# Order, pairing and banks of the probability-value products in two attention layers

## The chip, the cores and the metric

The kernel runs on one core of a Trainium2 chip. The metric is device time in microseconds (us) of one execution, from the start of the program to its end. Everything is one program: four layers of a first network (layers 0 to 3), then a second block ("mixers", then a feed-forward part), all for 256 latent and 256 context tokens of width 1024.

## What is computed

Layers 0 and 3 are a grouped-query attention with a window. Sixteen query heads of width 64 share four key/value heads; a block of 128 queries looks at up to 512 keys (256 of the context, 256 of the latent tokens). Cut to what the change touches:

```python
# reference, window_gqa_mixer (layers 0 and 3)
logits = jnp.einsum('bqkgd,bjkd->bkgqj', q_b, k_b).astype(jnp.float32) * scale
p = sink_softmax(jnp.where(mask, logits, NEG_INF), sink_l)
o = jnp.einsum('bkgqj,bjkd->bqkgd', p.astype(v_b.dtype), v_b)     # probabilities times values
y = (o * jax.nn.silu(z)) @ w_out
```

Layer 0 computes this for the context tokens (stream `c`, 256 keys) and the latent tokens (stream `l`, 512 keys); layer 3 for the latent tokens only. Everything is in float32.

## The kernel before, in words

**Order of work.** The program is written with a tile framework: the Python text gives a program order, and a scheduler at build time turns it into one fixed instruction list for each engine. At each step it takes, for an engine, the earliest instruction of the program order that is ready by its model; so work that stands later in the text (projections of the next group of heads, of the gate `z`, of the output, or of the next layer) is drawn forward into the gaps of work that stands earlier. On the chip each engine follows its list strictly and waits on semaphores.

**Attention of one layer.** `gqa` (L775 on) first projects keys, values and the first half of the queries, then calls `attend(0, ...)`, projects the second half of the queries, calls `attend(1, ...)`, then multiplies with the gate (`z_mul`, L737 on) and projects the output. `attend` loops over the streams, over two blocks of 128 queries (`q`), and over two key/value heads (`kv`) of the group `g`. For each `kv`:

- `softmax` (L860 on) writes the logits of four query heads into banks of the pool tag `S` (L876, L877; L880 adds the mask), takes the maximum (L881), the exponential (L889) and normalises (L897).
- For each tile of 128 keys (`j`; four for stream `l`, two for `c`), four transposes (L910) turn the probabilities of the four heads into a bank with tag `tp`; `evac` copies that bank to an SBUF tile `pT` (tag `T2`, three slots; ScalarE L704 and VectorE L708 in turn); two products (L915) multiply it with the values and add into the output bank `o`. The trace shows each product as two MATMUL instructions, and the tile `pT` under the name `T`.
- After both `kv`, `evac` copies `o` to the tile of `z` (named `Z` in the trace).

A product has 64 output columns of values, so its two heads of `i` go to the lower and the upper 64 partitions of `o`: in the trace these MATMULs have the shape `128*64`, all others around them `128*128`.

**Banks.** PSUM has eight banks here, shared out by tag: three `mm` (projections), two `S` (logits), three `tp` (transposes, the sums of the modulation weights at L518, and `o`). A projection fill is 48 matmuls of 256 columns or 24 of 512 (lines L377, L378 and L380, or L366 to L368) into one `mm` bank; a gate projection is then read once by ScalarE (L747) and once by VectorE (L748), after which its bank is free.

**Counts.** Layer 0: 2 groups x (2 blocks x 2 heads x 2 key tiles for `c` + 2 x 2 x 4 for `l`) = 48 tiles `pT`. Layer 3: 2 x 2 x 2 x 4 = 32. Together 80, with two products each.

Of the kernel before, what the change touches and what calls it, by code (L numbers as in the profile page):

```python
# [19 lines left out]
F32 = mybir.dt.float32  # L20
# [40 lines left out]
class Weight:  # L61


    def __init__(self, name, src, K, blocks, kstep, rows=None, pick=None):
        self.name, self.src, self.K, self.kstep, self.rows, self.pick = name, src, K, kstep, rows, pick
        self.blocks = blocks
        self.off = []
        off = 0
        KC = K // 128
        for cols in blocks:  # L70
            parts = []
            for k0 in range(0, KC, kstep):
                kc = min(kstep, KC - k0)
                parts.append((off, k0, kc, len(cols)))
                off += 128 * kc * len(cols)
            self.off.append(parts)
        self.size = off
# [191 lines left out]
class Net:  # L269
    def __init__(self, tc, A, out, stack, upto=99):  # L270
        self.tc, self.nc, self.A, self.out = tc, tc.nc, A, out
        self.upto = upto
        P = lambda name, bufs, **k: stack.enter_context(tc.tile_pool(name=name, bufs=bufs, **k))
        self.const = P("const", 1)
        self.res = P("res", 1)
        self.wp = P("wp", 2)
        self.tmp = P("tmp", 2)
        self.ps = P("ps", 2, space=PSUM)
        self.dram = P("dram", 1, space=bass.MemoryType.DRAM)
        self.open("act")  # L280
        self.flip = 0
        self.deep = 0
        self.filler = iter(())
        self.later = None
        self.n = 0
# [262 lines left out]
    def ada_all(self, mod, nxt):  # L548
        yield from self.ada_steps(mod, (2,))
        if nxt is not None:  # L550
            yield from self.ada_steps(nxt, (0, 1))

    def gates(self, mod, streams):

        G = self.t([128, 2, D], F32, "K8")
        out = {}
        for i, v in enumerate("lc"):
            if v in streams:
                self.bcast(G[:, i, :], mod["g"][i:i + 1, :], D)
                out[v] = G[:, i, :]  # L560
        return out
# [213 lines left out]
    def gqa(self, l, hT, mod, nxt, need_ctx, p0):  # L775
        nc = self.nc
# [9 lines left out]
        vt = self.t([128, 4, 256], F32, "V4")  # L786
# [111 lines left out]
            return P  # L898

        def attend(g, qs, z):  # L900
            for s in qstreams:
                nj = 4 if s == "l" else 2
                for q in range(2):
                    o = self.pt([128, 2, 2, 128], "tp")
                    for kv in range(2):
                        P = softmax(s, q, g, kv, qs)
                        for j in range(nj):
                            tp = self.pt([128, 4, 128], "tp")
                            for r in range(4):
                                nc.tensor.transpose(tp[:, r, :], P[r][:, j * 128:(j + 1) * 128], self.eye)  # L910
                            pT = self.t([128, 4, 128], F32, "T2")
                            self.evac(pT, tp)
                            vv = vt[:, j, (2 * g + kv) * 64:(2 * g + kv + 1) * 64]
                            for i in range(2):
                                nc.tensor.matmul(o[i * 64:(i + 1) * 64, kv], vv, pT[:, 2 * i:2 * i + 2, :],  # L915
                                                 start=j == 0, stop=j == nj - 1)
                    self.evac(z[s][:, :, q * 128:(q + 1) * 128], o.rearrange("p a b c -> p (a b) c"))

        z0 = self.z_new(qstreams)
        attend(0, q0, z0)  # L920
        p1 = self.load(name, 2)
        q1 = {s: queries(s, p1) for s in qstreams}
        z1 = self.z_new(qstreams)
        attend(1, q1, z1)
        y = self.halves(qstreams) if need_ctx else {"l": self.halves("c")["c"]}
        for g, z in enumerate((z0, z1)):
# [1101 lines left out]
```

## Time and profile before

| what | value |
|---|---|
| median of 3 runs | 1478.16 us (1475.01 to 1479.94) |
| the profiled execution | 1472.61 us |
| its span, first to last instruction | 1470.8 us |
| mean granted TensorE clock | 0.996 |
| PE (TensorE matmul) busy | 1433.8 us, 97% |
| DVE (VectorE) busy | 1046.3 us, 71% |
| ACT (ScalarE) busy | 737.2 us, 50% |
| DMA, share of 16 engines | 40.8% |

How to read it: PE is TensorE's multiplying, PEld its loading of weights, which runs beside it. A line number is that of the kernel before. Matmuls are pipelined: the next starts before the last one's end, so the "busy" time of single matmuls adds up to more than they cost. What a matmul costs in a stream is the step from its start to the next one's start, and that is how it is read here. A timeline row `start, duration, engine, line, ... xN` merges N instructions in a row of one line. The profiled execution lies 5.55 us below the median of the runs; a difference worked out in it is taken off the median.

### The profile page before, as it was taken

Reading aid. Unit: us, or ns where it says so; the run is one execution under the profiler, and the core shown is the slowest. Engines: PE = TensorE matmul, PEld = TensorE weight load, DVE = VectorE, ACT = ScalarE, POOL = GpSimd, SP = SyncE. Lnnn points to the kernel's source line nnn. Section 1 sums busy time; section 2 is a strip of 40 time slices with the busy share of each in tenths; the row PEclk is TensorE's granted clock in tenths of the full one; section 3 lists DMA queues with packets and bytes.
Section 4 is the critical chain, followed back from the end, with each engine's and each line's share of the span. In section 5 each row is a group of like instructions: output and inputs, shape, how many; then the busy total and the mean of one; then the engine's idle time right before and its main releaser. Section 6 shows DMA issues by size and latency. Waiting matters only on the chain.

```text
span 1470.8 us, 24541 instructions
## 1 busy us (share of the span) xinstructions
PE 1433.8 (97%) x9445; PEld 1171.0 (80%) x9445; DVE 1046.3 (71%) x2241; ACT 737.2 (50%) x1447; POOL 50.3 (3%) x72
## 2 busy tenths in 40 slices
PE   7999999999899999999999999999999999899998
PEld 4876677779687777787878777768988899799987
DVE  4678765553687666696585768889787887799963
ACT  4555543442456344364544535656575645466542
POOL 0000000000000000010000000000000000211100
PEclk9999999999999999999999999999999999999999
DMA  9601315552313325424323332246524444555552
GB/s 364 199 1 58 115 63 202 202 193 94 122 44 110 134 72 179 158 72 163 110 101 115 128 131 100 88 127 216 176 98 158 154 133 134 182 186 186 183 178 98
DMA packets 63555, 203.35 MB, mean 138 GB/s; under 512 B 10329, under 2 KB 14542, under 8 KB 63438
## 3 DMA queue, kind: packets, MB, share of 16 engines
q1 hardware_dynamic: 63438, 201.79, 40.8%
q8 instruction: 74, 1.21, 0.3%
q14 instruction: 43, 0.35, 0.1%
HBM read 200.65 MB, written 1.11 MB: 137 GB/s over the span
## 4 chain that ended last, share of the span: by engine, by line
PE 86%; DMA 5%; DVE 5%; ACT 2%; issue 1%; POOL 0%; SPq 0%; ACTq 0%; DVEq 0%; POOLq 0%
PE mm L366 11%; PE mm L368 11%; PE mm L367 11%; PE mm L377 8%; PE mm L378 7%; PE mm L380 7%; DMA ar<-in_w_l_ada_dram 3%; PE tp L518 3%; PE tp L915 3%; PE tp L910 3%; PE tp L712 2%; PE S L876 1%; PE S L380 1%; PE S L377 1%; PE S L378 1%
## 5 line engine op out<-in xcount | busy, mean ns | idle before, releaser
L347 DVE TENSOR_TENSOR wl<-wr,wh 128x1024 fp32r<-128x1024 f32 (+5 forms) x168 | 196.9, 1181 | 68.5 <-ACT wh L345 66.0
L345 ACT ACTIVATE wh<-wr 128x1024 fp32r<-128x1024 f32 (+5 forms) x172 | 174.6, 1026 | 90.6 <-PE mm L378 32.8
L377 PE MATMUL mm<-thl,wh 128*128 128x256 f32 x608 | 175.3, 289 | 1.3 <-ACT thl L661 1.3
L378 PE MATMUL mm<-tll,wh 128*128 128x256 f32 x608 | 173.5, 286 | 0.0
L380 PE MATMUL mm<-thl,wl 128*128 128x256 f32 x608 | 173.2, 286 | 0.0
L366 PE MATMUL mm<-wh,thl 128*128 128x512 f32 (+3 forms) x312 | 122.6, 393 | 1.4 <-ACT thl L661 1.0
L367 PE MATMUL mm<-wl,thl 128*128 128x512 f32 (+3 forms) x312 | 122.2, 392 | 0.0
L368 PE MATMUL mm<-wh,tll 128*128 128x512 f32 (+3 forms) x312 | 122.2, 392 | 0.0
L377 PEld LDWEIGHTS mm<-thl,wh 128*128 128x128 f32 x608 | 116.2, 191 | 4.2 <-issue 1.9
L378 PEld LDWEIGHTS mm<-tll,wh 128*128 128x128 f32 x608 | 116.3, 191 | 1.6 <-issue 1.2
L380 PEld LDWEIGHTS mm<-thl,wl 128*128 128x128 f32 x608 | 116.0, 191 | 0.7 <-issue 0.3
L368 PE MATMUL mm<-wh,tlc 128*128 128x512 f32 (+2 forms) x240 | 94.0, 394 | 0.3 <-DVE tlc L1886 0.3
L366 PE MATMUL mm<-wh,thc 128*128 128x512 f32 (+2 forms) x232 | 92.6, 399 | 1.6 <-DVE thc L595 1.6
L367 PE MATMUL mm<-wl,thc 128*128 128x512 f32 (+2 forms) x232 | 91.1, 394 | 0.0
L347 DVE TENSOR_TENSOR wl<-wrd,wh 128x1024 fp32r<-128x1024 f32 x52 | 65.9, 1269 | 27.5 <-ACT wh L345 27.4
L889 ACT ACTIVATE P<-S,nm 128x512 f32<-128x512 f32 (+1 forms) x96 | 58.6, 614 | 53.3 <-DVE nm L882 45.4
L366 PEld LDWEIGHTS mm<-wh,thl 128*128 128x128 f32 x312 | 58.7, 188 | 13.0 <-issue 1.6
L368 PEld LDWEIGHTS mm<-wh,tll 128*128 128x128 f32 x312 | 58.7, 188 | 10.8 <-issue 1.0
L345 ACT ACTIVATE wh<-wrd 128x1024 fp32r<-128x1024 f32 x52 | 53.6, 1050 | 26.6 <-PE mm L367 23.7
L367 PEld LDWEIGHTS mm<-wl,thl 128*128 128x128 f32 x312 | 58.7, 188 | 10.0 <-issue 0.8
L377 PE MATMUL mm<-thc,wh 128*128 128x256 f32 (+1 forms) x216 | 65.5, 303 | 0.1
L380 PE MATMUL mm<-thc,wl 128*128 128x256 f32 (+1 forms) x216 | 64.8, 300 | 0.0
(564 smaller groups left out, 3744.9 us busy)
## 6 DMA issues: line engine op xcount, KB each, us to landing
ar<-in_w_l_ada_dram SPq DMA_DIRECT2D x80, 512.0 KB
wr<-in_w_l_in_dram SPq DMA_DIRECT2D x48, 512.0 KB
wr<-in_w_l_out_dram SPq DMA_DIRECT2D x32, 512.0 KB
wr<-in_w_s_mg_dram SPq DMA_DIRECT2D x24, 512.0 KB
wrd<-in_w_s_down_dram SPq DMA_DIRECT2D x22, 512.0 KB
wrd<-in_w_s_gate_dram SPq DMA_DIRECT2D x20, 512.0 KB
wrd<-in_w_s_up_dram SPq DMA_DIRECT2D x20, 512.0 KB
wr<-in_w_s_br_dram SPq DMA_DIRECT2D x12, 512.0 KB
```

The lines of the kernel that those rows point to most:

```text
L345: nc.scalar.activation(hi[:, :kc * n], raw[:, :kc * n], AF.Copy)
L347: eng.tensor_sub(lo[:, :kc * n], raw[:, :kc * n], hi[:, :kc * n].bitcast(F32))
L366: nc.tensor.matmul(ps, xh(kk), wh[:, k, n0:n0 + n], start=kk == 0, stop=False)
L367: nc.tensor.matmul(ps, xh(kk), wl[:, k, n0:n0 + n], start=False, stop=False)
L368: nc.tensor.matmul(ps, xl(kk), wh[:, k, n0:n0 + n], start=False, stop=kk == KC - 1)
L377: nc.tensor.matmul(ps, wh[:, k, n0:n0 + m], xh(kk), start=kk == 0, stop=False)
L378: nc.tensor.matmul(ps, wh[:, k, n0:n0 + m], xl(kk), start=False, stop=False)
L380: nc.tensor.matmul(ps, wl[:, k, n0:n0 + m], xh(kk), start=False, stop=kk == KC - 1)
L518: nc.tensor.matmul(ps[32 * g:32 * g + 32, :], self.cs[:, k, :], r[:, g * 256:(g + 1) * 256], start=k == 0, stop=k == 7)
L889: nc.scalar.activation(p[:, :nk], ps[:, i, :], AF.Exp, scale=scale, bias=nm[:, r:r + 1], accum_out=sm[:, r:r + 1])
L910: nc.tensor.transpose(tp[:, r, :], P[r][:, j * 128:(j + 1) * 128], self.eye)
L915: nc.tensor.matmul(o[i * 64:(i + 1) * 64, kv], vv, pT[:, 2 * i:2 * i + 2, :], start=j == 0, stop=j == nj - 1)
```

## The change

`attend` no longer multiplies each tile `pT` right after it was copied. Key tiles are taken in pairs: four transposes and a copy for the first, the same for the second, and only then the products of the pair before (kept in the list `due`), which may belong to the previous head or the previous block of queries. The four products of a pair (eight MATMULs) go through a new helper `together`: the first is placed as usual, the other three are tied behind it and given high priority, so that the scheduler puts nothing between them. Within a pair the second tile is multiplied first. The copy of `o` to `z` moves behind the products that end it (`then`), and the last pair of a call of `attend` is multiplied at its end. The output bank `o` moves from tag `tp` to tag `mm`. Every fourth `pT` takes the single slot of tag `bb`, which layer 2 owns already, so four `pT` are available where there were three. The number of transposes, copies and products stays the same, and no DMA is added, removed or moved in the text.

```diff
--- before.py
+++ after.py
@@ -278,7 +278,7 @@
         self.ps = P("ps", 2, space=PSUM)
         self.dram = P("dram", 1, space=bass.MemoryType.DRAM)
         self.open("act")
-        self.flip = 0
+        self.flip = self.turned = 0
         self.deep = 0
         self.filler = iter(())
         self.later = None
@@ -550,6 +550,13 @@
         if nxt is not None:
             yield from self.ada_steps(nxt, (0, 1))
 
+    def together(self, work):
+
+        first = work[0]()
+        with self.tc.issue_after(first.ins), self.tc.high_priority():
+            for w in work[1:]:
+                w()
+
     def gates(self, mod, streams):
 
         G = self.t([128, 2, D], F32, "K8")
@@ -898,23 +905,44 @@
             return P
 
         def attend(g, qs, z):
+
+            due = []
+
+            def product():
+                o, kv, vs, pTs, first, last, then = due.pop()
+                n = len(pTs)
+                self.together([
+                    (lambda m=m, i=i: nc.tensor.matmul(o[i * 64:(i + 1) * 64, kv], vs[m], pTs[m][:, 2 * i:2 * i + 2, :],
+                                                       start=first and m == n - 1, stop=last and m == 0))
+                    for m in reversed(range(n)) for i in range(2)])
+                if then is not None:
+                    then()
+
             for s in qstreams:
                 nj = 4 if s == "l" else 2
                 for q in range(2):
-                    o = self.pt([128, 2, 2, 128], "tp")
+                    o = self.pt([128, 2, 2, 128], "mm")
+                    out = lambda s=s, q=q, o=o: self.evac(z[s][:, :, q * 128:(q + 1) * 128],
+                                                          o.rearrange("p a b c -> p (a b) c"))
                     for kv in range(2):
                         P = softmax(s, q, g, kv, qs)
-                        for j in range(nj):
-                            tp = self.pt([128, 4, 128], "tp")
-                            for r in range(4):
-                                nc.tensor.transpose(tp[:, r, :], P[r][:, j * 128:(j + 1) * 128], self.eye)
-                            pT = self.t([128, 4, 128], F32, "T2")
-                            self.evac(pT, tp)
-                            vv = vt[:, j, (2 * g + kv) * 64:(2 * g + kv + 1) * 64]
-                            for i in range(2):
-                                nc.tensor.matmul(o[i * 64:(i + 1) * 64, kv], vv, pT[:, 2 * i:2 * i + 2, :],
-                                                 start=j == 0, stop=j == nj - 1)
-                    self.evac(z[s][:, :, q * 128:(q + 1) * 128], o.rearrange("p a b c -> p (a b) c"))
+                        for j0 in range(0, nj, 2):
+                            pTs = []
+                            for j in (j0, j0 + 1):
+                                tp = self.pt([128, 4, 128], "tp")
+                                for r in range(4):
+                                    nc.tensor.transpose(tp[:, r, :], P[r][:, j * 128:(j + 1) * 128], self.eye)
+                                self.turned += 1
+                                pT = self.t([128, 4, 128], F32, "T2") if self.turned % 4 else self.t([128, 4, 128], F32, "bb", 1)
+                                self.evac(pT, tp)
+                                pTs.append(pT)
+                            if due:
+                                product()
+                            vv = slice((2 * g + kv) * 64, (2 * g + kv + 1) * 64)
+                            end = j0 + 2 == nj
+                            due.append((o, kv, [vt[:, j, vv] for j in (j0, j0 + 1)], pTs, j0 == 0, end,
+                                        out if end and kv == 1 else None))
+            product()
 
         z0 = self.z_new(qstreams)
         attend(0, q0, z0)
```

## Rows read from the trace of the kernel before

**Rows 1.** The page, busy time: engine, busy us (share of span) and instructions.
```profile
PE 1433.8 (97%) x9445; PEld 1171.0 (80%) x9445; DVE 1046.3 (71%) x2241; ACT 737.2 (50%) x1447; POOL 50.3 (3%) x72
```

**Rows 2.** The page, chain that ended last, share of the span by engine.
```profile
PE 86%; DMA 5%; DVE 5%; ACT 2%; issue 1%; POOL 0%; SPq 0%; ACTq 0%; DVEq 0%; POOLq 0%
```

**Rows 3.** Windows (us, then busy per engine, clock): attention of layers 0, 3; after it.
```profile
86.00:216.00 130.00, 129.93 (x913) 89.95 (x911) 99.19 (x256) 69.31 (x180) 0.00 (x0) 1.00 0.17 56
898.00:985.50 87.50, 87.09 (x595) 61.99 (x594) 73.45 (x159) 51.30 (x108) 0.00 (x0) 1.00 0.28 89
1000.00:1030.00 30.00, 28.72 (x170) 25.61 (x169) 27.45 (x76) 19.75 (x33) 0.39 (x2) 1.00 0.69 225
```

**Rows 4.** Groups by line, PE, products: busy us, mean ns | idle before; layer 0, 3.
```profile
L915 PE MATMUL tp<-T,V 128*64 128x256 f32 x192 | 30.0, 401 | 0.1
...
L915 PE MATMUL tp<-T,V 128*64 128x256 f32 x128 | 19.1, 398 | 0.1
```

**Rows 5.** Timeline of PE (start us, duration us, line): four products amid other work.
```profile
89.72 0.28 PE L380 MATMUL mm<-thc,wl 128*128 128x256 f32 x1
89.84 0.28 PE L377 MATMUL mm<-thc,wh 128*128 128x256 f32 x1
90.05 0.65 PE L915 MATMUL tp<-T,V 128*64 128x256 f32 x4
90.63 0.98 PE L910 MATMUL tp<-eye,P 128*128 128x128 f32 x7
```

**Rows 6.** Timeline of PE: eight products in a row, then 512-column matmuls.
```profile
102.06 0.28 PE L380 MATMUL mm<-thc,wl 128*128 128x256 f32 x1
102.27 1.08 PE L915 MATMUL tp<-T,V 128*64 128x256 f32 x8
103.28 0.50 PE L876 MATMUL S<-K,Q 128*128 128x512 f32 x1
103.62 0.39 PE L877 MATMUL S<-K,Q 128*128 128x512 f32 x1
```

**Rows 7.** Timeline of PE: eight transposes behind a matmul, and behind products.
```profile
100.12 1.03 PE L910 MATMUL tp<-eye,P 128*128 128x128 f32 x8
100.91 0.48 PE L876 MATMUL S<-K,Q 128*128 128x512 f32 x1
...
110.67 1.09 PE L910 MATMUL tp<-eye,P 128*128 128x128 f32 x8
111.51 0.48 PE L876 MATMUL S<-K,Q 128*128 128x512 f32 x1
```

**Rows 8.** Timeline of PE: the first group of products.
```profile
87.94 0.65 PE L915 MATMUL tp<-T,V 128*64 128x256 f32 x4
```

**Rows 9.** Waits (us in total, times, longest) of the products' weight loads; layer 0, 3.
```profile
PEld tp L915 <- ACT T L704: 3.2, 12, 0.4
...
PEld tp L915 <- ACT T L704: 2.4, 6, 0.6
```

**Rows 10.** Timeline of ACT and DVE: the slowest emptying of a projection's bank.
```profile
155.63 0.60 ACT L747 ACTIVATE mid<-mm 128x512 f32<-128x512 f32 x1
...
157.86 0.68 DVE L748 SCALAR_TENSOR_TENSOR mid<-mid,mm 128x512 f32<-128x512 f32 x1
```

**Rows 11.** Timeline of PE: the end of layer 3's attention, and the next wait.
```profile
982.52 0.39 PE L368 MATMUL mm<-Q,tlc 128*128 128x512 f32 x1
982.75 0.39 PE L366 MATMUL mm<-Q,thc 128*128 128x512 f32 x1
983.07 1.08 PE L915 MATMUL tp<-T,V 128*64 128x256 f32 x8
984.08 1.64 PE L1583 MATMUL tp<-eye,mid 8*128 8x8 f32 x24
...
1005.62 0.46 PE L366 MATMUL mm<-wh,thl 128*128 128x416 f32 x1 [1.04 <-ACT thl L661]
```

## Prediction, made before the changed kernel was run

> **What bounds the kernel now.** I read the page's busy table first, then the chain that ended last, then busy time by window over the two stretches in which products run, then the timeline of PE inside them. PE is busy 97% of the span [rows 1], and 86% of the chain that ended last is PE's [rows 2]. In the stretches of the attention, 86 to 216 us (layer 0) and 898 to 985.5 us (layer 3), it is busier still: 129.93 of 130 us and 87.09 of 87.5 us, at the full clock (granted 1.00, the 2.4 GHz level), while DVE is busy 76% (99.19 of 130) and 84% (73.45 of 87.5) [rows 3]. So in these stretches the time is the number of steps in PE's list times their price. A wait of another engine for PE costs nothing; a shorter list of PE counts.
>
> PE's stream also hardly ever waits for the products' inputs: PE's own idle time ahead of all products is 0.1 us in each stretch [rows 4]. The loads of their weights wait 3.2 + 2.4 = 5.6 us for the copy of a tile [rows 9], but loads run beside the multiplying, so that is a ceiling and not a cost.
>
> **What a group of products costs.** Busy shares hide the main point; the steps in the timeline show it. From the start of the matmul ahead of four products to the start of the transposes behind them are 90.63 - 89.84 = 0.79 us [rows 5]; with eight products between two such points it is 103.28 - 102.06 = 1.22 us [rows 6]. Four more products therefore cost 0.43 us. The matmul ahead costs 0.12 us when its like follows (89.84 - 89.72) [rows 5]. So one group, whatever its length, costs 0.79 - 0.43 - 0.12 = 0.24 us on top of its products. Eight transposes take 0.79 us behind a matmul and 0.84 us behind products: 0.05 us more [rows 7]. Together 0.29 us per group. Where a 512-column matmul follows instead, its step is 103.62 - 103.28 = 0.34 us [rows 6] against 0.23 us in a plain stream (982.75 - 982.52) [rows 11]: then the group costs 0.24 + 0.11 = 0.35 us. In the timeline 46 of the groups have transposes behind them, so I take 0.30 us and keep 0.29 and 0.35 as ends.
>
> Products now come in 66 groups: 52 of four MATMULs and 14 of eight (320 in all), 42 of them in layer 0 and 24 in layer 3; the first and the last are shown [rows 8, 11].
>
> **The change, part by part.** *Removed: groups.* 80 tiles in pairs are 40 packs of eight MATMULs: 24 in layer 0, 16 in layer 3. The helper ties a pack together and its latest input (the second tile) is its first operand, so nothing in it waits; I take the packs as whole. Layer 0 loses 42 - 24 = 18 groups, 18 x 0.30 = 5.4 us; layer 3 loses 24 - 16 = 8, 2.4 us. Sum 26 x 0.30 = 7.8 us (7.5 to 9.1 with the ends). If a few packs touch (the last one of a call of `attend` follows its predecessor closely, four times), up to four groups or 1.2 us more go.
>
> *Removed: the wait of products for the copy of their tile.* Bounded by 0.1 us per stretch (PE's own idle time) and 5.6 us (the loads'); I take 0, since PE's row is the nearer, and keep 1 us for the range.
>
> *Moved: products behind the next pair's transposes.* What now stands behind a pack on PE are the following transposes, at most 1.01 us later (eight products, 102.27 to 103.28 [rows 6]). Copies wait for a free `pT`; with four slots instead of three two pairs fit. I cost it at nothing: PE is covered by projections drawn forward, as now. With the cover gone each end of a call shows a pack and a copy, 1.01 us and 0.60 us (the time of a copy of that shape on ACT) [rows 6, 10]. In layer 0 gate projections run on after the attention, in layer 3 the output projection does: after the last group at 983.07 PE goes on without a wait until 1005.62 [rows 11].
>
> *Moved: `o` from `tp` to `mm`.* Transposes get a third bank: worth nothing where PE never idles. Projections keep two banks while an `o` is live. A fill is 48 steps of 0.12 us, 5.7 us at least [rows 5]; the slowest emptying of its bank took 155.63 to 158.54, 2.9 us [rows 10]. So the other bank is empty again before the fill ends, and I take 0. The ends: 0, and one plain emptying (0.60 + 0.68 us [rows 10]) shown at each of the 18 fills of queries and gates behind the first call (12 in layer 0, 6 in layer 3): 23 us.
>
> *Unchanged:* copies, exponentials, maxima. No DMA moves in the text, and no queue of SP or POOL is passed.
>
> *Where the gain goes.* Layer 0's 5.4 us: PE stays the bound behind it, so all of it counts. Layer 3's 2.4 us run into a stretch where DVE is busy 27.45 of 30 us and PE waits 1.04 us for ACT [rows 3, 11]; I count 1.6 us of it, with 0 and 2.4 as ends. Sum 5.4 + 1.6 = 7.0 us. The profiled execution took 1472.61 us, 5.55 us less than the median of the runs, 1478.16; the same 7.0 us off the median give 1471.2 us. Its own range is 1467 to 1474 (11.3 us off, with ends, touching packs and waits; 4.2 us off, with layer 3's part lost and 1.2 us of ends shown).
>
> **A rule of the Trainium skill that speaks against it.** The fills and emptyings above say that two banks suffice. The Trainium skill (Perfetto Trace Analysis, Optimizing Tensor Performance, Matmuls) asks that independent groups rotate through different banks, so that the emptying of one runs under the next; taking a bank away goes against that. By the rows the rule stays met with two banks and costs 0; were it broken at each fill, it would be the second rival.
>
> **The rivals.**
>
> *The gain is swallowed.* The packs form, but the softmax chain sets the pace, or the new order leaves PE idle elsewhere. For it: DVE at 84% in layer 3 [rows 3]. Against it: 76% in layer 0, and fills left over behind both stretches. Half of the 7.0 us or more would be lost: 1475 to 1479, about 1477 us. That the packs don't form (the scheduler leaves some 66 groups) ends there too, at 1478; the ties in the helper speak against it.
>
> *Slower: projections starve for banks.* `o` sits in an `mm` bank over two heads, a second `mm` bank waits for ACT and DVE, and the fill that should cover PE cannot start. It decides from a mean wait of 7.0 / 18 = 0.39 us per fill. One full emptying at each is 18 x 1.28 = 23 us, 1494 us; with half of it covered by the attention's own matmuls 1478.2 - 7.0 + 11.5 = 1483 us, which I take. Against it: 5.7 us of fill against 2.9 us of emptying, and an `o` is written only now and then.
>
> *Much faster.* The 0.30 us is the wait for the copy and no price of the group; then standing behind the next pair hides it for all: 66 x 0.30 = 19.8 us, 1458 us. Against it: four products take the same 0.65 us at both places shown [rows 5, 8], and the transposes behind a group, which wait for no copy of it, carry part of the price [rows 7]. The Trainium skill (TensorEngine Tiling (Array Packing), Key Properties) says that a change of tiling mode drains TensorE; by that rule the price belongs to the change from 128 to 64 columns and back, and the trace agrees (0.30 us per group of any length).
>
> **How the numbers follow.** Forecast 0.58, swallowed or not formed 0.26, slower 0.13, much faster 0.03. A difference of 0.3%, 4.4 us, is about what a measurement of this kernel can tell from no change. Faster by more: 0.58 + 0.03 = 0.61; within: 0.26; slower by more: 0.13. The range 1465 to 1480 holds the forecast with 2 us for runs' scatter below it and nearly all of the swallowed case (0.58 + 0.24); the starved case and the very fast one are left out.
>
> **What would show it.** In the timeline after, the products stand in about 40 groups of eight (or fewer, longer ones), and the two stretches from the first to the last group shrink by about 5 and 2 us with PE still busy over 99%. Steps at a group's edges stay at 0.29 to 0.35 us. The prediction is wrong if there are more than 50 groups, if PE's idle time in the two stretches exceeds 2 us, if projections' first matmuls wait for L747 or L748, or if layer 3's end moves up and the mixers do not.

## The result, and the profile after

| | before | after |
|---|---|---|
| median, lowest and highest | 1476.59 us (1472.54 to 1479.94, 4 runs) | 1525.70 us (1523.51 to 1527.62, 4 runs) |
| ratio, 95% interval | 1 | 1.0333 [1.0299, 1.0367] |
| span of the profiled execution | 1470.8 us | 1525.8 us |
| mean granted TensorE clock | 0.996 | 0.981 |
| groups of products | 66 | 31 (22 of eight MATMULs, 9 of sixteen) |

The change makes the kernel 3.3% slower. The forecast was 1471.2 us, its range 1465 to 1480; it was wrong. The products did get together, more than forecast (31 groups, not 40), and yet the time grew by 49 us. Lines moved a little in the changed text: L876, L881, L889, L897, L910 of before are L883, L888, L896, L904, L934 of after; L704/L708 (the copies) are L711/L715; the products are L915 in both.

The page of after, busy time and the chain that ended last (answers to [rows 1] and [rows 2]):

```profile
span 1525.8 us, 24553 instructions
PE 1448.3 (95%) x9445; PEld 1187.1 (78%) x9445; DVE 1049.0 (69%) x2241; ACT 736.6 (48%) x1447; POOL 50.1 (3%) x72
...
PE 81%; DVE 8%; DMA 6%; ACT 3%; issue 2%; POOL 0%; SPq 0%; ACTq 0%; DVEq 0%; POOLq 0%
```

The count of instructions of each engine is what it was, so no work was added. The span grew by 55.0 us in two parts: PE idles 1525.8 - 1448.3 = 77.5 us where it idled 1470.8 - 1433.8 = 37.0 us, which is 40.5 us more; and the same 9445 matmuls are busy for 14.5 us more. DVE's share of the chain rose from 5% to 8%, ACT's from 2% to 3%.

What PE waited for, whole execution of after (engine, tag, line <- what it waited for: us in total, times, longest):

```profile
PE S L883 <- ACT P L896: 20.7, 21, 3.0
...
PE tp L934 <- DVE P L904: 5.0, 6, 1.4
...
PE tp L934 <- ACT T L711: 2.2, 4, 0.7
```

The first line did not exist before. Logits (L883) wait for a bank of `S`, which is free when the exponentials (L896) have read it: 21 waits, 20.7 us. The other two are waits of transposes, for the normalisation (L904) and for a copy (L711); before, the only one of either kind was a single wait of 0.2 us for the normalisation. These three lines are 27.9 us of the 40.5, and all of them lie inside the softmax chain. The projections do not wait: no line has an `mm` fill waiting for the emptying of a gate's bank, which is what my second rival foresaw.

PE in after, by window, in the attention of layer 0 and of layer 3 (us, then busy per engine with instructions, granted clock, DMA share, GB/s; answers to [rows 3]):

```profile
86.00:110.00 24.00, 17.29 (x97) 11.70 (x97) 16.81 (x57) 12.76 (x43) 0.00 (x0) 0.86 0.00 1
110.00:130.00 20.00, 17.76 (x110) 11.73 (x111) 15.45 (x41) 8.99 (x25) 0.00 (x0) 0.92 0.00 1
130.00:150.00 20.00, 19.96 (x173) 15.54 (x170) 7.70 (x18) 5.64 (x14) 0.00 (x0) 1.00 0.26 90
...
960.00:980.00 20.00, 14.52 (x61) 8.65 (x60) 15.34 (x37) 9.70 (x23) 0.00 (x0) 0.66 0.26 80
```

In before PE was busy for all but 0.07 us of the first stretch and 0.41 us of the second, at clock 1.00 [rows 3]. Now PE is busy 17.29 of 24 us, and no other engine has taken its place: DVE is at 16.81 of 24. No engine is full; PE and the softmax chain take turns. From 130 us on PE is full again while DVE falls to 7.70 of 20. So work that used to lie beside the softmax now lies behind it.

The same windows for one line of the projections alone (L377; first after, then before) show which work that is:

```profile
86.00:110.00 24.00, 0.00 (x0) 0.86 0.00 1
110.00:130.00 20.00, 0.00 (x0) 0.92 0.00 1
130.00:150.00 20.00, 8.56 (x29) 1.00 0.26 90
```

```profile
86.00:110.00 24.00, 5.06 (x17) 1.00 0.00 1
...
130.00:150.00 20.00, 3.11 (x11) 1.00 0.39 125
```

Before, 17 of its matmuls stood between 86 and 110 us, amid the attention; after, none does until 132.78 us, and then 29 of them come within 20 us. The timeline of PE in after shows both sides (start us, duration us, line, then the wait ahead of it in brackets):

```profile
100.74 1.08 PE L915 MATMUL mm<-T,V 128*64 128x256 f32 x8 [0.48 <-DVE T L715]
101.75 0.50 PE L883 MATMUL S<-K,Q 128*128 128x512 f32 x1
...
104.05 0.65 PE L915 MATMUL mm<-bb,V 128*64 128x256 f32 x4
104.53 0.60 PE L915 MATMUL mm<-T,V 128*64 128x256 f32 x4
106.17 0.50 PE L883 MATMUL S<-K,Q 128*128 128x512 f32 x1 [1.03 <-ACT P L896]
106.50 0.40 PE L884 MATMUL S<-K,Q 128*128 128x512 f32 x1
106.74 0.23 PE L887 MATMUL S<-mask,eyeb 128*128 128x128 bf16 x1
106.86 0.50 PE L883 MATMUL S<-K,Q 128*128 128x512 f32 x1
107.20 0.39 PE L884 MATMUL S<-K,Q 128*128 128x512 f32 x1
107.43 0.23 PE L887 MATMUL S<-mask,eyeb 128*128 128x128 bf16 x1
109.38 0.50 PE L883 MATMUL S<-K,Q 128*128 128x512 f32 x1 [1.72 <-ACT P L896]
...
110.15 0.79 PE L883 MATMUL S<-K,Q 128*128 128x512 f32 x1
110.74 1.48 PE L934 MATMUL tp<-eye,P 128*128 128x128 f32 x6
...
129.69 1.08 PE L915 MATMUL mm<-T,V 128*64 128x256 f32 x8
130.60 0.60 PE L915 MATMUL mm<-bb,V 128*64 128x256 f32 x4
131.03 0.60 PE L915 MATMUL mm<-T,V 128*64 128x256 f32 x4
131.56 0.51 PE L883 MATMUL S<-K,Q 128*128 128x512 f32 x1
...
132.78 0.36 PE L377 MATMUL mm<-thc,wh 128*128 128x256 f32 x1
```

In [rows 5] and [rows 6] matmuls of L377 and L380 stand right ahead of the products. Here there is nothing between two attention steps, and PE stands still for 1.03 and 1.72 us. Behind these waits the clock falls to its lower level (1.2 GHz; the mean granted clock is 0.63 in 109 to 112 us): the step from L883 to the next matmul is 0.33 us at 106.17 and 0.59 us at 110.15 (to 110.74). A clock of 0.981 over 1525.8 us is 2 x 0.019 x 1525.8 = 58 us at half speed; before it was 2 x 0.004 x 1470.8 = 12 us. In most of that time PE is busy: 47.3 us in after, 9.9 us in before. Half of the 37.4 us more, 18.7 us, is an estimate of what the lower clock adds to the busy time, and it covers the 14.5 us seen.

To place the loss I compared the two traces by equal work: the time at which PE has done the same amount of matmul (each matmul counted by its columns) in one and in the other. After is 24 us late at the end of layer 0's attention (14 us of that already at the point that before reaches at 86 us, in the first softmax ahead of the products), still 23 us late through layers 1 and 2, and 55 us late at the end of layer 3's attention and from then on. The whole loss lies in the two attentions.

### The profile page after: what moved, and what is told of

Its sections match the earlier page's. It is cut to its first block, busy times and chain, and to the rows that moved or that the text cites. A ratio compares the mean times of both kernels' runs of the same rounds, so it can differ in the third digit from the quotient of the medians.

```text
span 1525.8 us, 24553 instructions
## 1 busy us (share of the span) xinstructions
PE 1448.3 (95%) x9445; PEld 1187.1 (78%) x9445; DVE 1049.0 (69%) x2241; ACT 736.6 (48%) x1447; POOL 50.1 (3%) x72
## 4 chain that ended last, share of the span: by engine, by line
PE 81%; DVE 8%; DMA 6%; ACT 3%; issue 2%; POOL 0%; SPq 0%; ACTq 0%; DVEq 0%; POOLq 0%
PE mm L366 11%; PE mm L368 10%; PE mm L367 10%; PE mm L377 8%; PE mm L380 7%; PE mm L378 7%; DMA ar<-in_w_l_ada_dram 4%; PE tp L518 3%; PE mm L915 3%; PE tp L934 2%; PE tp L719 2%; PE S L883 2%; PE S L380 1%; PE S L377 1%; PE S L378 1%
## 5 line engine op out<-in xcount | busy, mean ns | idle before, releaser
L347 DVE TENSOR_TENSOR wl<-wr,wh 128x1024 fp32r<-128x1024 f32 (+5 forms) x168 | 196.7, 1182 | 77.8 <-ACT wh L345 72.5
L377 PE MATMUL mm<-thl,wh 128*128 128x256 f32 x608 | 173.7, 286 | 1.3 <-ACT thl L668 1.3
L380 PE MATMUL mm<-thl,wl 128*128 128x256 f32 x608 | 172.7, 285 | 0.0
L377 PEld LDWEIGHTS mm<-thl,wh 128*128 128x128 f32 x608 | 116.2, 191 | 3.7 <-issue 1.6
L380 PEld LDWEIGHTS mm<-thl,wl 128*128 128x128 f32 x608 | 116.0, 191 | 1.3 <-issue 0.7
L896 ACT ACTIVATE P<-S,nm 128x512 f32<-128x512 f32 (+1 forms) x96 | 58.6, 614 | 61.2 <-DVE nm L889 55.1
L347 DVE TENSOR_TENSOR wl<-wrd,wh 128x1024 fp32r<-128x1024 f32 x52 | 65.9, 1270 | 27.1 <-ACT wh L345 27.0
L888 DVE TENSOR_REDUCE mx<-S 128x1 f32<-128x512 f32 (+1 forms) x80 | 54.5, 687 | 26.7 <-PE S L887 23.0
L883 PE MATMUL S<-K,Q 128*128 128x512 f32 (+1 forms) x96 | 46.3, 490 | 21.8 <-ACT P L896 20.7
```

The lines of the kernel that those rows point to most:

```text
L347: eng.tensor_sub(lo[:, :kc * n], raw[:, :kc * n], hi[:, :kc * n].bitcast(F32))
L377: nc.tensor.matmul(ps, wh[:, k, n0:n0 + m], xh(kk), start=kk == 0, stop=False)
L380: nc.tensor.matmul(ps, wl[:, k, n0:n0 + m], xh(kk), start=False, stop=kk == KC - 1)
L883: nc.tensor.matmul(ps[:, i, :], qq, kh[:, kvh, :nk], start=True, stop=False)
L888: nc.vector.reduce_max(mx[:, r0:r0 + per], ps, axis=AX)
L896: nc.scalar.activation(p[:, :nk], ps[:, i, :], AF.Exp, scale=scale, bias=nm[:, r:r + 1], accum_out=sm[:, r:r + 1])
```

## The theories, and the experiments

**The order of the banks (theory A).** Banks of one tag are given out in the order of the text. `o` stands in `attend`; the projections that the scheduler used to draw forward (queries of the second group, the gates) stand behind that call. If `o` asks for an `mm` bank, no projection behind it can have one until the last `o` of that call has its own. So nothing is left to draw forward, and PE idles. By this theory the number of banks is beside the point.

**Too few banks (theory C).** Two `mm` banks, while `o` holds the third, are not enough for the projections (the rival of the prediction). One more bank cures it.

**Late products (theory B).** Standing behind the next pair's transposes, the products come late, copies wait for a free `pT`, and PE with them.

**o back in `tp`, all else as in after.**

```diff
-                    o = self.pt([128, 2, 2, 128], "mm")
+                    o = self.pt([128, 2, 2, 128], "tp")
```

> The changed kernel with one thing undone: the output bank o is back in tag tp. Theory A (bank order: the scheduler hands out the banks of one tag in the order of the text, so projections that stand behind attend in the text cannot get an mm bank before the last o of the call has its own): the projections come back between the products, PE idle in both stretches under 2 us, 30 groups of products instead of 66, so 36 x 0.30 = 10.8 us below the kernel before, about 1466 us. Theory B (putting products off and giving them priority starves PE, the bank doesn't matter): about 1525 us as the changed kernel. Theory C (two mm banks beside o are too few): as A, about 1466 us.

Measured: 1473.30 us against 1474.48 us of before beside it, ratio 0.9997 [0.9984, 1.0010], with 30 groups of products. PE's wait for the exponentials:

```profile
PE S L883 <- ACT P L896: 1.9, 2, 1.7
```

1.9 us are left of 20.7. The place of `o` is the whole loss, and late products fall as a cause of it. But the gain of 36 fewer groups, 36 x 0.30 = 10.8 us by my price, isn't there either, though theories A and C foresaw about 1466 us.

**Only o moved to `mm`, all else as in before.**

```diff
-                    o = self.pt([128, 2, 2, 128], "tp")
+                    o = self.pt([128, 2, 2, 128], "mm")
```

> The kernel before with one thing changed: o in tag mm; products stay right behind their tile's copy, no pairs, no ties. Theory A (bank order): no projections between the products of a call, PE idle and the lower clock as in the changed kernel, 1510 to 1535 us. Theory B (deferral and priority): as before, 1477 us. Theory C (two mm banks are too few): 1510 to 1535 us.

Measured: 1541.80 us, ratio 1.0449 [1.0407, 1.0490]. One word costs 67 us, more than the whole change. Its waits and, for L377 alone, its first window:

```profile
PE S L876 <- ACT P L889: 27.7, 27, 2.7
```

```profile
86.00:110.00 24.00, 0.00 (x0) 0.86 0.00 1
```

The picture is that of after: no fill amid the attention, and logits that wait for exponentials. Theory B foresaw 1477 us and falls; A and C foresaw the same loss (1510 to 1535 us), so this run doesn't tell them apart.

**o in a bank of its own, and one bank fewer for projections:** in after, then in before. Both have two banks for projections at all times, and `o` no longer stands in their row.

```diff
-BANKS = {"mm": 3, "S": 2, "tp": 3}
+BANKS = {"mm": 2, "S": 2, "tp": 3, "o": 1}
...
+                    o = self.pt([128, 2, 2, 128], "o")
```

> The changed kernel with o in a tag of its own with one bank; mm keeps two banks all through the program. Theory A (bank order): projections no longer stand behind an o in their tag, they come back, about 1467 to 1475 us (34 groups, 32 x 0.30 = 9.6 us less than before, and perhaps some us lost to two mm banks elsewhere). Theory B: about 1525 us. Theory C (two banks are too few): 1510 us or more.

> The kernel before with o in a tag of its own with one bank, mm with two, tp with three; products as before. Theory A (bank order): not slower than 1480; 43 groups of products for 66 since transposes get a third bank, 23 x 0.30 = 6.9 us less, about 1470 us. Theory B: 1477 us. Theory C (two mm banks are too few): 1510 us or more.

Measured: 1499.29 us, ratio 1.0177 [1.0154, 1.0200], and 1500.39 us, ratio 1.0184 [1.0160, 1.0207]. The first has 23 matmuls of L377 in its first window, where before has 17:

```profile
86.00:110.00 24.00, 6.64 (x23) 1.00 0.01 2
```

With the same eight banks, `o` apart from the projections' is 1525.7 - 1499.3 = 26.4 us faster in after (some 23 us by the two ratios, since these two were timed beside different runs of before) and 1541.8 - 1500.4 = 41.4 us in before. That speaks for theory A, but both times lie between its figures (at most 1475 and 1480 us) and theory C's (1510 us or more). What remains, about 25 us, isn't in the attentions: by equal work the first of the two kernels is level with before (0.4 us ahead) at the end of layer 0's attention, 28 us late ahead of layer 3's and 27 us late at the end: it loses in layers 1 and 2, which have only two `mm` banks now as well. So a bank fewer does cost, but elsewhere.

**The same number of banks, shared or apart:** `o` alone with three `mm` banks, against four `mm` banks that `o` shares. Both leave two banks to `tp`.

```diff
-BANKS = {"mm": 3, "S": 2, "tp": 3}
+BANKS = {"mm": 3, "S": 2, "tp": 2, "o": 1}
...
-                    o = self.pt([128, 2, 2, 128], "mm")
+                    o = self.pt([128, 2, 2, 128], "o")
```

> The changed kernel with o in a tag of its own with one bank, mm with three and tp with two. Theory A (bank order): the projections stand between the products again (they do in the built instruction list: 291 and 229 of them in the two stretches against 183 and 77 in the changed kernel), and with three mm banks the 25 us that the two other own-bank kernels lost outside the attention stay away as far as they came from mm; what two tp banks cost the other layers is not known. About 1470 us for the stretches alone, up to 1500 if two tp banks cost as much elsewhere as two mm banks did. Theory C (the number of mm banks beside o): about 1467 us. Theory B (deferral): 1525 us.

```diff
-BANKS = {"mm": 3, "S": 2, "tp": 3}
+BANKS = {"mm": 4, "S": 2, "tp": 2}
```

> The changed kernel (o in mm) with four mm banks and two tp banks, so that three mm banks are free beside an o. Theory A (bank order): a bank more changes nothing, since the first projection behind attend still comes after the last o of the call in the order of the tag: about 1525 us or somewhat more, PE idle in both stretches. Theory C (too few banks): the projections come back, 1465 to 1480 us.

Measured: 1495.60 us, ratio 1.0151 [1.0130, 1.0172], and 1558.38 us, ratio 1.0578 [1.0532, 1.0623]. This pair decides between A and C. If banks were too few, four `mm` banks would cure the loss; they gave the slowest kernel of all (two runs, 1553.92 and 1562.84 us), 62.8 us behind the one that has the same four banks with `o` apart. Its first window, L377 alone, and its first wait in the attention:

```profile
86.00:110.00 24.00, 0.00 (x0) 0.86 0.00 1
```

```profile
PE S L883 <- ACT P L896: 20.0, 24, 2.2
```

By equal work it loses 35 us in layer 0's attention, 21 us in layer 1 and 33 us in layer 3's attention. Layer 1's part is that of two `tp` banks: the kernel with `o` apart loses 26 us there (from 5 us ahead of before to 21 us behind), and nothing in the attentions.

The order on PE says the same without any time. A call of `attend` has 96 product MATMULs in layer 0 and 64 in layer 3, and its last `o` gets its first product as number 65 and number 33. Counted in PE's timeline of after, no other matmul into an `mm` bank stands between the products of the four calls until 80, 80, 48 and 48 of them are done; with only `o` moved it is 76, 72, 44 and 44, with four `mm` banks 80, 72, 48 and 48. In every kernel with `o` elsewhere the first one comes after 4 to 16 products. So in all twelve calls the projections stay behind the last `o`'s first product, as theory A has it.

**Without the fourth slot for pT, o in `tp`.** Why was the first experiment no faster than before?

```diff
-  pT = self.t([128, 4, 128], F32, "T2") if self.turned % 4 else self.t([128, 4, 128], F32, "bb", 1)
+  pT = self.t([128, 4, 128], F32, "T2")
```

> o in tag tp, pairs, ties and putting off as in the change, but three slots for pT instead of four (no tile in tag bb). 40 groups of products in the built list, none longer than a pack. If the fourth slot is worth something (packs meet, copies wait less), this is slower than the run with o in tp by up to 10 x 0.30 = 3 us, 1473 to 1477 us; if not, the same within noise.

Measured: 1471.27 us, ratio 0.9992 [0.9980, 1.0003], 40 groups. The slot makes no difference that can be told.

**Pairs, but not put off: the products right behind their own pair's copies, o in `tp`.** The call moves from ahead of `due.append` to behind it, in the loop.

```diff
-                            if due:
-                                product()
...
-            product()
+                            product()
```

> o in tag tp, pairs and ties as in the change, but the products of a pair stand right behind their own copies in the text. The built list has 41 groups of products against 30 in the run with o in tp (25 and 16 in the two layers). If putting off is what swallowed the saving of that run, this one is faster: 25 groups fewer than before x 0.30 = 7.5 us, about 1467 us. If the saving goes to waits for the modulation weights and for the softmax chain whatever the order, 1470 to 1475 us.

Measured: 1467.30 us against 1472.75 us, ratio 0.9960 [0.9948, 0.9972], 41 groups: faster than both kernels. Pairing pays, and with `o` in `tp` putting off behind the next pair takes it away again. By equal work the gain is 4.7 us at the end of layer 0's attention, where 42 - 25 = 17 groups are gone: 0.28 us a group. In the first experiment layer 0 has 24 groups fewer and gains 4.0 us, and layer 3 gains nothing; the waits among its logits (1.9 us, against 0.5 us here) are one part. PE's matmuls are busy for as long in both (1426.1 and 1425.9 us); what differs is PE's idle time. The two stretches of the attention in the first experiment, then in this one:

```profile
86.00:216.00 130.00, 127.10 (x941) 95.32 (x940) 101.00 (x261) 69.34 (x181) 0.00 (x0) 1.00 0.17 58
898.00:985.50 87.50, 84.83 (x590) 63.67 (x589) 72.97 (x163) 50.49 (x108) 0.00 (x0) 1.00 0.27 90
```

```profile
86.00:216.00 130.00, 129.13 (x941) 94.60 (x942) 101.76 (x259) 68.39 (x179) 0.00 (x0) 1.00 0.21 69
898.00:985.50 87.50, 86.82 (x588) 64.78 (x584) 73.82 (x164) 51.33 (x107) 0.00 (x0) 1.00 0.30 96
```

PE idles 2.90 + 2.67 = 5.57 us in the first experiment and 0.87 + 0.68 = 1.55 us here (before: 0.07 + 0.41). These 4.0 us are most of the 1469.5 - 1464.7 = 4.8 us between the two spans. In the first experiment they are one wait of 2.65 us for the DMA of modulation weights (L518), 1.9 us of waits for exponentials, and 0.72 us for projection weights (L347); these are single executions, and why the order brings these waits is not shown. Putting off alone does not: the kernel with `o` apart and three `mm` banks puts off too, and PE idles 1.0 us between its first and last products of the two layers.

**All key tiles of a softmax together, o in `tp`, not put off.**

```diff
-                        for j0 in range(0, nj, 2):
+                        for j0 in range(0, nj, nj):
...
-                            for j in (j0, j0 + 1):
+                            for j in range(nj):
...
-                            due.append((o, kv, [vt[:, j, vv] for j in (j0, j0 + 1)], pTs, j0 == 0, end,
+                            due.append((o, kv, [vt[:, j, vv] for j in range(nj)], pTs, j0 == 0, end,
```

> The run before with pairs not put off (41 groups of products, o in the transposes' tag, 1467.3 us), with one step more: the products of all key tiles of one softmax (two or four) stand behind the copies of all of them, so that each product group has 4 or 8 matmuls of 128x256 and there are 24 groups. If the price of a group (0.30 us) is what the packing saves, and the PE finds projections to run while the four copies are made, 17 groups fewer are 5.1 us: 1462 us, ratio 0.993. If the products then wait for the last of the four copies (2.5 to 3 us for four copies on two engines, and four pT tiles held until the products have run, so that the next softmax's copies wait), up to 24 waits of 0.3 us or more take it back: 1467 to 1475 us, with waits of transposes for DVE and ACT in the list of waits.

Measured: 1461.20 us against 1473.90 us, ratio 0.9914 [0.9886, 0.9942], 24 groups (8 of eight, 16 of sixteen): the fastest. PE in 86 to 216 us:

```profile
86.00:216.00 130.00, 129.95 (x967) 97.77 (x966) 101.67 (x263) 68.67 (x182) 0.00 (x0) 1.00 0.21 71
```

```profile
177.20 0.65 PE L915 MATMUL tp<-bb,V 128*64 128x256 f32 x4
177.69 1.46 PE L915 MATMUL tp<-T,V 128*64 128x256 f32 x12
179.08 0.39 PE L380 MATMUL mm<-thc,wl 128*128 128x256 f32 x1
```

PE is as full as before [rows 3] and has started 967 matmuls in the stretch, before 913. PE waits 0.2 us in all for a copy ahead of products, although four copies stand ahead of them. By equal work this trace is 6.8 us ahead at the end of layer 0's attention with 42 - 16 = 26 groups fewer: 0.26 us a group. From the ratios, 66 - 24 = 42 groups fewer make 0.0086 x 1473.9 = 12.7 us, 0.30 us a group (0.20 to 0.40 us by the ends of the interval). (Its profiled execution was the slowest of its five runs, 1468.49 us, so the ratio comes from the timed runs.)

## Why the prediction was wrong, step by step

- *PE bounds the attention.* Right for the kernel before, and in after the cause of the loss: PE was full only because projections stood between the steps of the softmax. I took "busy 129.93 of 130 us" [rows 3] as a property of the stretch. It came from what the scheduler had to fill it with.
- *A group costs 0.30 us.* Right in kind and near in size. In after eight products and their way out take 101.75 - 100.74 = 1.01 us, as in [rows 6] (103.28 - 102.27), and sixteen take 131.56 - 129.69 = 1.87 us: eight more cost 0.86 us, twice the 0.43 us of the sum. In the two kernels with products not put off a group saved was worth 0.24 us (0.0040 x 1472.75 us over 25 groups) and 0.30 us by the timed runs, and 0.19 to 0.28 us by equal work in single layers. The gain went with the number of groups; the products are the same 320. The Trainium skill (TensorEngine Tiling (Array Packing), Key Properties) says that a change of tiling mode drains TensorE. The runs agree with that sentence, but none of them changes the mode alone, so that the price comes from there is not shown.
- *26 groups go.* Under-counted: 35 went, because packs of neighbouring pairs touch. The fourth slot for `pT` lets them: with `o` in `tp` and fills between the products there are 30 groups, and 40 without that slot.
- *Products moved behind the next pair cost nothing.* With `o` in `tp`, wrong by the size of the gain: with it 0.9997, without it 0.9960. The reason given, "PE is covered by projections drawn forward, as now", fails altogether in after, where none is drawn forward. The nearest row I had was the copy's wait of a few tenths [rows 9], and that said nothing on what the new order does to the list.
- *`o` from `tp` to `mm` costs 0, at most 23 us.* This is the step that failed. Moved alone it cost 67 us, and together with the rest all of the loss. I asked whether two banks keep up with filling (5.7 us) and emptying (2.9 us [rows 10]). They do: no fill waits for an emptying in after, nor in the stretches of the changed kernel with `o` apart and two `mm` banks, where fills do stand amid the products (in before with `o` apart there is one such wait, of 0.7 us). What I did not ask is who stands ahead of whom for a bank. The projections could be drawn past `attend` because `attend` needed no `mm` bank. That later work "is drawn forward into the gaps" has a condition that I overlooked: it must be able to have its bank before the earlier work has its own.
- *Layer 3's gain half swallowed.* Not to be told in after, which loses 32 us there. In the kernel with pairs not put off layer 3 gained about 2 us by equal work, near the 2.4.
- *The rivals.* "Projections starve for banks" named the right place and the right victim, and had a chance of 0.13. Its mechanism (a fill waiting for the emptying) and its price (1483 us, at most 1494) were both wrong: the starving happens when the list is built and not on the chip, so the trace of after shows it as waits of the softmax and not of the fills. The question that would have priced it is what PE has left to do in the attentions if no fill is drawn into them. The Trainium skill's advice (Perfetto Trace Analysis, Optimizing Tensor Performance, Matmuls) to rotate through different banks is for independent groups. Four `mm` banks with `o` among them gave 1.0578, and the same banks with `o` apart 1.0151: groups that stand behind `o` in the order of one tag are not independent in that sense.
- *What would show it.* Of the four signs named, PE's idle time over 2 us in the two stretches showed (24 - 17.29 = 6.71 us in the first 24 us alone, 16.1 and 9.5 us between the first and last products of the two layers); fills that wait for L747 or L748 did not.

What stays open: the runs show that the projections stay behind the last `o` of a call; that the banks of a tag are given out in text order is read from this, not seen in the scheduler itself. Open, too, is why putting the products off, with `o` in `tp`, costs its 0.4%, some 5.5 us. PE's idle time in the two stretches holds 4.0 us of it, but why the order brings these waits is not shown. Whether the loss in after could be cured with `o` in `mm` by moving the projections ahead of `attend` in the text was not tried.

## What to carry to other kernels

Before a long-lived tile is moved to another tag, list who asks for that tag later in the text and is drawn forward today: in this framework a tile that waits for its data barred all of these from the tag's banks, with three banks and with four. An engine that is 100% busy in a stretch may be so only by such filler, so cost a change by what it lets the scheduler still move as well as by waits on the chip. Putting small products together was worth 0.2 to 0.3 us for each group that went, 12.7 us in the best kernel here, with nothing else moved.

## What the runs showed of the chip

The clock fell where PE's work came with holes, and matmuls at the lower clock took longer. After in layer 3, by windows of 3 us:

```profile
956.00:959.00 3.00, 3.00 (x16) 2.54 (x16) 2.83 (x3) 2.70 (x4) 0.00 (x0) 1.00 0.18 52
959.00:962.00 3.00, 1.96 (x9) 1.01 (x8) 2.94 (x7) 0.50 (x1) 0.00 (x0) 1.00 0.84 279
962.00:965.00 3.00, 2.09 (x7) 1.07 (x7) 2.72 (x7) 2.19 (x5) 0.00 (x0) 0.69 0.05 22
965.00:968.00 3.00, 1.33 (x3) 0.64 (x3) 2.92 (x4) 1.59 (x3) 0.00 (x0) 0.50 0.54 175
...
974.00:977.00 3.00, 3.00 (x15) 2.55 (x14) 1.42 (x4) 0.87 (x2) 0.00 (x0) 0.53 0.00 0
977.00:980.00 3.00, 3.00 (x24) 1.57 (x22) 1.90 (x7) 1.84 (x6) 0.00 (x0) 1.00 0.00 0
```

PE was full up to 959 us at 1.00 (2.4 GHz), idled a third of the next 3 us, and the clock went to 0.50 (1.2 GHz) and stayed there until PE was full again. I had counted no clock cost at all in the prediction.
